# Writing the low part of the dense stages' weight tiles on the vector engine

## The chip, the cores and the metric

The kernel runs on one core of a Trainium2 chip. The metric is the device time of one execution in microseconds (us), the median of several runs. An engine's instructions run in the order in which they stand in its own queue. Between engines they wait on semaphores. PE is the matrix engine (PEld its weight loads), DVE the vector engine, ACT the scalar engine, POOL the GpSimd engine, SP the queue that issues most DMAs.

## The reference

Two layers over 16 learned tokens and 1024 input tokens, width 1024. Layer 0 mixes with multi-head latent attention (16 heads), layer 1 with a causal pooling mixer over windows of 2, 4, 8 and 16 tokens. Each mixer and each gated MLP (inner width 2816) is wrapped in RMS norms. All is float32.

```python
for i in range(DEPTH):
    a = rmsnorm(h, norm_mix_pre[i])
    if i % N_MIXERS == 0:
        m = mla_mixer(a, ...)
    else:
        m = pool_mixer(a, pool_w_group[j], pool_scale[j])
    h = h + rmsnorm(m, norm_mix_post[i])
    f = conv_ffn(rmsnorm(h, norm_ffn_pre[i]), ffn_w_up[i], ffn_conv_w[i], ffn_conv_b[i], ffn_w_down[i])
    h = h + rmsnorm(f, norm_ffn_post[i])
```

In `conv_ffn` an up-projection is followed by a causal depthwise convolution of width 3, `silu(gate) * val`, and a down-projection.

## The kernel before, in words

A matmul reads its operands as `float32r`, which keeps fewer bits than float32. So each float32 operand is split in two: a high part, which is the value rounded to `float32r`, and a low part, which is the value minus the high part. A product is three matmuls: high by high, high by low, low by high. `split` (line 60) makes the two parts. ACT writes the high part (a cast, line 64), and the engine named by `lo_eng` writes the low part with a subtraction (line 70).

The program has two stages. `mla` (the first 550 us or so) computes the latent projections and the attention. `dense` then does the output projection `wo`, the MLP of layer 0, the pooling mixer, and the MLP of layer 1. The 1040 tokens are handled in two halves of 536 and 504 columns (hf 0 and hf 1). Activations stand with the features on the 128 partitions, so the weights are the stationary operand of each matmul.

All weights of `dense` come through `wtile` (line 702). It loads up to 1024 columns of float32 weights into a `wr` tile (three buffers) by a DMA on SP, and splits them into `wh` and `wl` (four buffers each). A tile's `wh` takes the buffer of the tile four before it, so the cast on ACT waits for PE, and the subtraction waits for the cast. `mm_half` (line 744) issues the matmuls (line 756). A half of 536 columns is cut into two matmuls of 268, so a full weight tile is 48 matmuls there and 24 for the half of 504.

In `ffn_up` (line 878) the output of a tile in PSUM is convolved: one ACT pass (line 899), two DVE passes (line 903), then the product of gate and value (line 909) and a split into `gh` and `gl` whose low part is DVE's. In layer 0 with hf 0 the norm's scale comes late, so DVE first copies the PSUM tile times that scale into `u` (line 895). For hf 0 the PSUM pool holds three such tiles, for hf 1 six.

The norms run beside the matmuls as generators in a list `bg`, which `tick` advances between tiles. `post` (line 817) multiplies the eight tiles `F` of a sub-layer's output by gain and scale (line 824), adds them to the residual `H` (line 829), and sums the squares into `acc` (`addsq`, lines 778 and 779). `inv_rms_a` reduces `acc` over the partitions by small matmuls into `ps_st` (line 82), DVE takes the reciprocal root in some dozen tiny instructions (lines 84 to 99), DVE and POOL each write a `diag` tile (line 115), and PE spreads the scale over the partitions into `ps_bc` (line 122), which ACT copies out as `R`. `pre` (line 839) makes the split inputs `ah` and `al` of the next MLP. `poolmix` (line 973) runs four groups of window sums (`pa`, `psm`, `pmx`, lines 988 to 1005), splits the result into `xh` and `xl`, and multiplies by small weights `pwh` and `pwl`, which `wtile` also makes.

The order of the instructions on each engine isn't written by hand: the tile framework's scheduler places each instruction by priority and by its own timeline of when its operands are there. `ahead` lowers a priority number so that norms and mixers go first.

Of the kernel before, what the change touches and what calls it, by code (L numbers as in the profile page):

```python
# [46 lines left out]
class Kern:  # L47
# [654 lines left out]
    def wtile(self, src, nk, pool=False):  # L702
        nc = self.nc
        n = 128 * nk
        r = self.wp.tile([128, 1024], F32, tag="wr", name="wr", bufs=3)
        if pool:
            hi = self.wp.tile([128, 512], F32R, tag="pwh", name="pwh", bufs=1)
            lo = self.wp.tile([128, 512], F32R, tag="pwl", name="pwl", bufs=1)
        else:
            hi = self.wp.tile([128, 1024], F32R, tag="wh", name="wh")  # L710
            lo = self.wp.tile([128, 1024], F32R, tag="wl", name="wl")
        src = src if isinstance(src, list) else [src]
        for i, a in enumerate(src):
            w = n // len(src)
            nc.sync.dma_start(r[:, i * w:i * w + w], a)
        self.split(r[:, :n], hi[:, :n], lo[:, :n])
        return [(hi[:, 128 * k:128 * k + 128], lo[:, 128 * k:128 * k + 128]) for k in range(nk)]

    @staticmethod
# [354 lines left out]
```

## Time and profile before

| | |
|---|---|
| median of 3 runs | 2288.43 us (2287.2 to 2289.56) |
| the profiled execution, its own time | 2289.22 us |
| its span in the trace | 2287.4 us |
| PE busy | 2172.8 us (95%) |
| DVE busy | 1333.4 us (58%) |
| POOL busy | 1124.3 us (49%) |
| ACT busy | 1046.3 us (46%) |
| mean granted PE clock | 0.974 |

Busy time is the union of an engine's instructions, without its register and semaphore work. Durations and waits below come from this one execution; between its span and its own time lie 1.8 us outside the traced instructions.

### The profile page before, as it was taken

The numbers are of one execution on the slowest core, as the hardware profiler recorded it, in microseconds if no ns is written. First come the engines' busy times: TensorE is split into PE (matmuls) and PEld (weight loads), VectorE is DVE, ScalarE is ACT, GpSimd is POOL, SyncE is SP. The second block draws the span as 40 slices with busy tenths as digits, with TensorE's granted clock in tenths as the row PEclk, the third lists the DMA queues.
The fourth block names the chain that finished last, engine by engine and source line by source line (L and its number), as shares of the span: only waits on it lengthen the run. The fifth ranks groups of instructions, "written<-read, shape, count | busy, mean of one in ns | idle before, by whom it ended". The sixth has DMA issues, their size and how long they took to land.

```text
span 2287.4 us, 36601 instructions
## 1 busy us (share of the span) xinstructions
PE 2172.8 (95%) x13968; PEld 1983.4 (87%) x13968; DVE 1333.4 (58%) x2506; ACT 1046.3 (46%) x1934; POOL 1124.3 (49%) x1079
## 2 busy tenths in 40 slices
PE   8889999998989999999998999999899999999996
PEld 8878889887978999999787788899899998888886
DVE  7867777776389614754985534486733347421334
ACT  6456777775454323343443444344334333433431
POOL 5657676765533344444443544444343344444442
PEclk9989999998999999999999999999999999999998
DMA  5011111114343223223222422322242234323231
GB/s 160 16 42 25 32 32 32 26 55 131 120 140 115 85 88 102 89 81 128 80 80 75 149 98 82 130 79 84 60 139 93 79 118 159 113 82 113 96 92 46
DMA packets 82904, 202.77 MB, mean 89 GB/s; under 512 B 10548, under 2 KB 31668, under 8 KB 82728
## 3 DMA queue, kind: packets, MB, share of 16 engines
q1 hardware_dynamic: 82584, 200.18, 27.9%
q8 instruction: 110, 1.80, 0.3%
q14 instruction: 66, 0.54, 0.1%
q10 hardware_dynamic: 144, 0.25, 0.0%
HBM read 179.15 MB, written 16.97 MB: 86 GB/s over the span
## 4 chain that ended last, share of the span: by engine, by line
PE 75%; DVE 13%; ACT 4%; issue 3%; POOL 2%; DMA 2%; SPq 0%; DVEq 0%; ACTq 0%; POOLq 0%
PE ps_m L756 62%; DVE acc L779 2%; PE ps_t L577 2%; DVE cv L903 2%; DVE F L824 1%; PE ps_s L525 1%; PE ps_o L562 1%; PE ps_s L527 1%; PE ps_s L526 1%; DVE H L829 1%; PE ps_o L563 1%; ACT P L540 1%; PE ps_qk L408 1%; DVE psm L998 1%; PE ps_st L82 1%
## 5 line engine op out<-in xcount | busy, mean ns | idle before, releaser
L70 POOL TENSOR_TENSOR wl<-wr,wh 128x1024 fp32r<-128x1024 f32 (+3 forms) x316 | 702.4, 2223 | 891.8 <-ACT wh L64 879.4
L756 PE MATMUL ps_m<-al,wh 128*128 128x506 f32 (+2 forms) x2112 | 569.9, 324 | 0.0
L756 PE MATMUL ps_m<-ah,wh 128*128 128x506 f32 (+2 forms) x2112 | 566.2, 322 | 3.4 <-DVE cv L903 2.5
L756 PE MATMUL ps_m<-ah,wl 128*128 128x506 f32 (+2 forms) x2112 | 566.2, 322 | 0.0
L64 ACT CAST wh<-wr 128x1024 fp32r<-128x1024 f32 (+3 forms) x316 | 300.4, 951 | 502.5 <-PE ps_m L756 351.4
L903 DVE SCALAR_TENSOR_TENSOR cv<-ps_m,params,cv 128x504 f32<-128x504 f32 (+1 forms) x264 | 196.4, 746 | 360.7 <-ACT cv L899 357.1
L756 PEld LDWEIGHTS ps_m<-ah,wh 128*128 128x128 f32 x2112 | 355.5, 191 | 34.2 <-ACT sq L778 2.7
L756 PEld LDWEIGHTS ps_m<-al,wh 128*128 128x128 f32 x2112 | 355.1, 190 | 29.2 <-issue 1.5
L756 PEld LDWEIGHTS ps_m<-ah,wl 128*128 128x128 f32 x2112 | 355.6, 190 | 27.6 <-issue 0.2
L756 PE MATMUL ps_m<-gh,wh 128*128 128x268 f32 (+3 forms) x1088 | 290.4, 319 | 5.0 <-ACT F L765 5.0
L756 PE MATMUL ps_m<-gl,wh 128*128 128x268 f32 (+3 forms) x1088 | 289.7, 319 | 0.0
L756 PE MATMUL ps_m<-gh,wl 128*128 128x268 f32 (+3 forms) x1088 | 289.2, 318 | 0.0
L756 PEld LDWEIGHTS ps_m<-gh,wh 128*128 128x128 f32 x1088 | 184.3, 191 | 19.1 <-ACT F L765 5.2
L756 PEld LDWEIGHTS ps_m<-gh,wl 128*128 128x128 f32 x1088 | 183.6, 190 | 14.3 <-issue 0.5
L756 PEld LDWEIGHTS ps_m<-gl,wh 128*128 128x128 f32 x1088 | 183.6, 190 | 13.4 <-issue 0.2
L64 ACT CAST gh<-cv 128x504 fp32r<-128x504 f32 (+2 forms) x88 | 54.8, 623 | 224.8 <-DVE cv L909 224.8
L779 DVE TENSOR_TENSOR acc<-acc,sq 128x536 f32<-128x536 f32 (+4 forms) x97 | 109.9, 1137 | 50.9 <-ACT sq L778 47.8
L545 POOL TENSOR_SCALAR P<-P,stat 116x116 f32<-116x116 f32 (+2 forms) x144 | 108.7, 756 | 59.2 <-DVE stat L543 47.5
L903 DVE SCALAR_TENSOR_TENSOR cv<-u,params,cv 128x535 f32<-128x535 f32 x88 | 112.4, 1278 | 41.5 <-ACT cv L899 40.2
L907 ACT ACTIVATE cv<-cv 128x504 f32<-128x504 f32 (+2 forms) x88 | 55.9, 635 | 166.8 <-DVE cv L903 166.7
L540 ACT ACTIVATE P<-ps_s,stat 116x116 f32<-116x116 f32 (+9 forms) x160 | 111.3, 698 | 37.5 <-DVE stat L538 26.3
L577 PE MATMUL ps_t<-ident,P 116*116 116x116 f32 x720 | 117.6, 267 | 6.1 <-DVE ptl L591 2.7
(200 smaller groups left out, 3732.9 us busy)
## 6 DMA issues: line engine op xcount, KB each, us to landing
wr<-in_w_up SPq DMA_DIRECT2D x176, 512.0 KB, 3.5
wr<-in_w_down SPq DMA_DIRECT2D x56, 384.0 KB, 3.1
wr<-in_w_down SPq DMA_DIRECT2D x56, 320.0 KB, 2.9
wr<-in_w_o SPq DMA_DIRECT2D x16, 512.0 KB, 3.5
resid<-H SPq DMA_DIRECT2D x16, 268.0 KB, 2.5
H<-resid SPq DMA_DIRECT2D x16, 268.0 KB, 2.8
xt<-in_x SPq DMA_DIRECT2D x32, 130.0 KB, 2.3
resid<-H SPq DMA_DIRECT2D x16, 252.0 KB, 2.4
```

What stands on the lines that cost most here:

```text
L64: nc.scalar.copy(hi, src)
L70: eng.tensor_tensor(lo, src, hi.bitcast(F32), op=ALU.subtract)
L82: nc.tensor.matmul(ps[:w, i:i + 1], acc[:, w * i:w * i + w], self.ones, start=True, stop=True)
L408: nc.tensor.matmul(ps, wh, xh, start=i == 0, stop=False)
L525: nc.tensor.matmul(ps[:n, x, :w], qh[:, qs], kh[:, ks], start=True, stop=False)
L540: nc.scalar.activation(dst, ps, AF.Exp, bias=nm[:n], scale=SCALE, accum_out=es[:n, gi:gi + 1])
L545: nc.gpsimd.tensor_scalar(P[:n, :nk], P[:n, :nk], rs[:n], 1.0, op0=ALU.mult, op1=ALU.mult)
L577: nc.tensor.transpose(pt[:kn, x * QT:x * QT + n], Pi[:n, k0:k0 + kn], self.ident[:n, :n])
L756: nc.tensor.matmul(p, w, x[k][:, skip + c0:skip + c0 + m], start=k == 0 and w is wh and x is xh, stop=k == last and w is wl)
L779: (eng or nc.vector).tensor_tensor(acc, acc, sq[:, :n], op=ALU.add)
L903: nc.vector.scalar_tensor_tensor(c[:, o:], u[:, pad + x - 2 + o:pad + x - 2 + n], self.par(p0 + x), c[:, o:], op0=ALU.mult, op1=ALU.add)
L907: nc.scalar.activation(c, c, AF.Silu)
```

## The change

`wtile` asks `split` for DVE in place of POOL as the engine of the subtraction. This holds for all 324 weight tiles of `dense`: 316 `wl` and 8 `pwl`. The operands, buffers and the arithmetic stay as they are. The other calls of `split`, those of the attention among them, stay as they are too.

```diff
@@ -713,7 +713,7 @@
         for i, a in enumerate(src):
             w = n // len(src)
             nc.sync.dma_start(r[:, i * w:i * w + w], a)
-        self.split(r[:, :n], hi[:, :n], lo[:, :n])
+        self.split(r[:, :n], hi[:, :n], lo[:, :n], lo_eng="dve")
         return [(hi[:, 128 * k:128 * k + 128], lo[:, 128 * k:128 * k + 128]) for k in range(nk)]
```

The scheduler orders the dense stage anew on every engine. Three places follow.

On DVE, the `post` of hf 0 after `wo`, from the tile `diag` to the first rows of `acc`. `F`, `H`, `al` and `acc` are the norm's tiles; the two widths of `acc` belong to the two halves. Before:

```order
L115 TENSOR_TENSOR diag<-ident,yh 67x536
L824 SCALAR_TENSOR_TENSOR F<-F,params,R 128x536 x8
L829 TENSOR_TENSOR H<-H,F 128x536 x8
L866 SCALAR_TENSOR_TENSOR al<-H,params,ah 128x536 x3
L779 TENSOR_TENSOR acc<-acc,sq 128x504
L866 SCALAR_TENSOR_TENSOR al<-H,params,ah 128x536 x5
```

and in the change:

```order
L115 TENSOR_TENSOR diag<-ident,yh 67x536
L70 TENSOR_TENSOR wl<-wr,wh 128x1024
L824 SCALAR_TENSOR_TENSOR F<-F,params,R 128x536 x8
L829 TENSOR_TENSOR H<-H,F 128x536
L70 TENSOR_TENSOR wl<-wr,wh 128x1024
L829 TENSOR_TENSOR H<-H,F 128x536 x7
L70 TENSOR_TENSOR wl<-wr,wh 128x1024
L866 SCALAR_TENSOR_TENSOR al<-H,params,ah 128x536 x3
L779 TENSOR_TENSOR acc<-acc,sq 128x504
L866 SCALAR_TENSOR_TENSOR al<-H,params,ah 128x536
L70 TENSOR_TENSOR wl<-wr,wh 128x1024
L866 SCALAR_TENSOR_TENSOR al<-H,params,ah 128x536 x2
```

From `F` to the last `acc` of this chain six `wl` stand among the norm's instructions now, where none stood, and one more behind it.

On PE, the place where the same chain's `acc` is reduced (`ps_st`, line 82). Before, it stands between the last matmuls of `wo` (`oh`, `ol`) and the first of `ffn_up` (`ah`, `al`):

```order
L756 MATMUL ps_m<-oh,wh 128x504
L756 MATMUL ps_m<-ol,wh 128x504
L756 MATMUL ps_m<-oh,wl 128x504
L82 MATMUL ps_st<-ones,acc 67x1 x8
L756 MATMUL ps_m<-ah,wh 128x268 x2
```

and in the change:

```order
L756 MATMUL ps_m<-ah,wl 128x268 x2
L756 MATMUL ps_m<-ah,wh 128x268 x2
L756 MATMUL ps_m<-al,wh 128x268 x2
L82 MATMUL ps_st<-ones,acc 67x1 x8
L756 MATMUL ps_m<-ah,wl 128x268 x2
```

The reduction moved behind 52 matmuls of `ffn_up`, one weight tile and four matmuls. The next reduction but one (hf 1, `63x1`) moved from the 971st to the 1168th line 756 matmul.

On DVE, the first group of the pooling mixer of hf 0. Before:

```order
L903 SCALAR_TENSOR_TENSOR cv<-ps_m,params,cv 128x504
L998 TENSOR_TENSOR psm<-pa 128x551
L909 TENSOR_TENSOR cv<-cv 128x504
L1001 SCALAR_TENSOR_TENSOR pmx<-psm,pa 128x536
L988 SCALAR_TENSOR_TENSOR pa<-H,params,R 128x536
L1004 TENSOR_TENSOR pmx<-psm,params 128x16
L70 TENSOR_TENSOR gl<-cv,gh 128x504
```

and in the change:

```order
L70 TENSOR_TENSOR gl<-cv,gh 128x504
L998 TENSOR_TENSOR psm<-pa 128x551
L70 TENSOR_TENSOR wl<-wr,wh 128x1024
L1001 SCALAR_TENSOR_TENSOR pmx<-psm,pa 128x536
L988 SCALAR_TENSOR_TENSOR pa<-H,params,R 128x536
L903 SCALAR_TENSOR_TENSOR cv<-ps_m,params,cv 128x504
L1004 TENSOR_TENSOR pmx<-psm,params 128x16
```

A `wl` now stands between the window sum and the `pmx` that the mixer's matmuls wait for.

## Rows read from the trace of the kernel before

**Rows 1.** Page of the profile: span, and busy time of each engine.

```profile
span 2287.4 us, 36601 instructions
PE 2172.8 (95%) x13968; PEld 1983.4 (87%) x13968; DVE 1333.4 (58%) x2506; ACT 1046.3 (46%) x1934; POOL 1124.3 (49%) x1079
```

**Rows 2.** Busy time by stretches: start:end, length, engines (count), PEclk, DMA share, GB/s.

```profile
640.00:740.00 100.00, 86.08 (x620) 81.99 (x618) 85.33 (x131) 45.48 (x67) 42.27 (x17) 0.91 0.34 116
740.00:1090.00 350.00, 350.00 (x2763) 346.19 (x2762) 182.96 (x193) 128.41 (x169) 149.43 (x86) 1.00 0.31 96
1090.00:1290.00 200.00, 185.54 (x865) 153.90 (x864) 150.17 (x218) 87.95 (x140) 97.83 (x58) 0.96 0.30 94
1290.00:1465.00 175.00, 175.00 (x765) 143.98 (x764) 76.06 (x99) 70.90 (x96) 77.23 (x37) 1.00 0.34 108
1465.00:1690.00 225.00, 210.15 (x1585) 200.68 (x1584) 154.69 (x224) 90.74 (x133) 92.96 (x52) 0.96 0.28 86
1690.00:2250.00 560.00, 560.00 (x3302) 499.55 (x3301) 204.32 (x271) 208.98 (x277) 249.32 (x131) 1.00 0.32 104
2250.00:2288.00 38.00, 18.77 (x164) 17.43 (x162) 23.62 (x76) 5.61 (x14) 5.82 (x8) 0.74 0.17 55
```

**Rows 3.** What PE waited for, 590 to 2288 us: total, times, longest, us.

```profile
PE ps_st L82 <- DVE acc L779: 20.6, 5, 8.3
PE ps_m L756 <- ACT xh L64: 10.9, 2, 6.8
```

**Rows 4.** Lines by form, POOL: out<-in, shapes, count | busy us, mean ns | idle before, releaser.

```profile
L70 POOL TENSOR_TENSOR wl<-wr,wh 128x1024 fp32r<-128x1024 f32 x196 | 478.9, 2444 | 590.0 <-ACT wh L64 580.1 <-DMA resid<-H 9.6
L70 POOL TENSOR_TENSOR wl<-wr,wh 128x768 fp32r<-128x768 f32 x56 | 115.8, 2069 | 178.6 <-ACT wh L64 178.6
```

**Rows 5.** Lines by form, DVE (and ACT's cast of the widest weight tile).

```profile
L903 DVE SCALAR_TENSOR_TENSOR cv<-ps_m,params,cv 128x504 f32<-128x504 f32 x176 | 129.9, 740 | 241.4 <-ACT cv L899 239.0
L903 DVE SCALAR_TENSOR_TENSOR cv<-u,params,cv 128x535 f32<-128x535 f32 x44 | 76.3, 1734 | 40.2 <-ACT cv L899 40.2
L903 DVE SCALAR_TENSOR_TENSOR cv<-u,params,cv 128x534 f32<-128x534 f32 x44 | 36.2, 823 | 1.2
L779 DVE TENSOR_TENSOR acc<-acc,sq 128x536 f32<-128x536 f32 x42 | 57.9, 1379 | 32.0 <-ACT sq L778 30.6
L829 DVE TENSOR_TENSOR H<-H,F 128x536 f32<-128x536 f32 x24 | 15.4, 705 | 0.0
L534 DVE CUSTOM_DVE_ANT_0 ps_s<-ps_s,mask 116x928 f32<-116x928 f32 x16 | 18.0, 1128 | 2.7 <-PE ps_s L527 1.3 <-POOL P L545 0.5 <-PE ps_o L563 0.4
L64 ACT CAST wh<-wr 128x1024 fp32r<-128x1024 f32 x196 | 205.5, 1048 | 266.5 <-PE ps_m L756 186.4 <-issue 54.4 <-POOL wl L70 18.0
```

**Rows 6.** Timeline, DVE and then POOL, 622 to 662 us: start us, us, instructions merged.

```profile
622.28 9.88 DVE L824 SCALAR_TENSOR_TENSOR F<-F,params,R 128x536 f32<-128x536 f32 x8 [6.50 <-ACT R L124]
632.08 5.09 DVE L829 TENSOR_TENSOR H<-H,F 128x536 f32<-128x536 f32 x8
...
645.36 14.79 DVE L779 TENSOR_TENSOR acc<-acc,sq 128x504 f32<-128x504 f32 x12
...
623.27 2.72 POOL L70 TENSOR_TENSOR wl<-wr,wh 128x1024 fp32r<-128x1024 f32 x1 [3.80 <-ACT wh L64]
...
654.80 2.60 POOL L70 TENSOR_TENSOR wl<-wr,wh 128x1024 fp32r<-128x1024 f32 x1 [0.17 <-ACT wh L64]
```

**Rows 7.** Timeline, PE, 640 to 672 us: the reduction and the matmuls around it.

```profile
649.33 0.39 PE L756 MATMUL ps_m<-oh,wl 128*128 128x504 f32 x1
658.03 1.97 PE L82 MATMUL ps_st<-ones,acc 128*67 128x1 f32 x16 [8.31 <-DVE acc L779]
```

**Rows 8.** Busy time by stretches, 100 us of layer 0's `ffn_up`, hf 0.

```profile
800.00:900.00 100.00, 100.00 (x812) 100.00 (x812) 24.18 (x23) 31.00 (x41) 42.73 (x22) 1.00 0.31 93
```

**Rows 9.** Busy time by stretches of `wl` alone (PE, PEld, POOL with counts).

```profile
1090.00:1290.00 200.00, 94.50 (x237) 45.92 (x236) 83.58 (x35) 0.96 0.30 94
1465.00:1690.00 225.00, 103.06 (x487) 78.25 (x488) 78.57 (x36) 0.96 0.28 86
```

## The prediction

> **What bounds the kernel now.** I read the page first, then the busy time by stretches, then what PE waited for, then the lines by form, and last the timeline around the longest wait. The page shows PE busy for 95% of the span [rows 1]. In the dense stage the stretches split cleanly: in 740 to 1090, 1290 to 1465 and 1690 to 2250 us PE is busy all the time at clock 1.00 [rows 2]. Nothing that DVE or POOL do there can shorten the kernel. All the dense stage's loss but its tail lies in three stretches where norms and mixers run: 640 to 740, 1090 to 1290 and 1465 to 1690 us. PE sits idle there for 13.9, 14.5 and 14.9 us, and the mean granted clock falls to 0.91, 0.96 and 0.96, so a part of each ran at the lower of the clock's two levels, 1.2 GHz in place of 2.4 [rows 2]. The clock's shares are 9, 8 and 9 us. So these stretches offer at most 22.9 + 22.5 + 23.9 = 69 us.
>
> DVE is busy for 85%, 75% and 69% of them [rows 2], and PE's longest waits name DVE: 20.6 us for `acc` at `ps_st`, 10.9 us for the mixer's `xh`, which ACT casts from DVE's `pmx` [rows 3].
>
> The lines by form then show what slows DVE. The addition `acc` takes 1379 ns on average; the addition `H`, with the same shape and also all in SBUF, takes 705 [rows 5]. The pass of `cv` that reads `u` from SBUF takes 1734 ns, the one behind it 823, and the one that reads PSUM 740. The timeline says why: a DVE instruction with both inputs in SBUF that starts under a POOL `wl` ends when the `wl` ends, and those that read PSUM run on. In 622 to 660 us the eight `F` take 9.9 us, the eight `H`, under no `wl` but one's end, 5.1 us, and twelve `acc` 14.8 us, under `wl` of 2.4 to 3.0 us [rows 6].
>
> **The change, part by part.** *What goes from POOL:* 316 `wl` at 2444 ns for the widest and 2069 for 768 columns [rows 4], and 8 `pwl`. POOL isn't the bound, so its time itself is worth nothing; what counts is the hold on DVE. By groups: `acc` 42 x (1379 - 705) = 28 us, `cv` from `u` 44 x (1734 - 823) = 40 us [rows 5]. The smaller groups look alike, and I estimate 150 us in all.
>
> *What comes to DVE:* no row shows this subtraction on DVE at 1024 columns. From above, 1024/536 times `H`'s 705 ns gives 1347 ns. From below, the 928 columns of the masked maximum take 1128 ns [rows 5], so it isn't under that. Between lies the line through these two points, 705 + (1128 - 705)/392 x 488 = 1232 ns; I take 1.23 us, since 928 is the nearest width. On the same line 768 columns cost 0.96 and 640 cost 0.82 us. The sum is 196 x 1.23 + 56 x 0.96 + 56 x 0.82 = 341 us, and some 14 us for the 16 other tiles: 355 us. DVE's busy time should go from 1333 to about 1333 - 150 + 355 = 1540 us.
>
> *The steady stretches.* A weight tile of 48 matmuls of 268 columns takes PE 48 x 100/812 = 5.9 us [rows 8], and of 24 wide ones about as long (765 matmuls in 175 us, 5.5 us [rows 2]). One more instruction of 1.23 us per tile leaves DVE at some 50 to 75%. `wl` needs the cast, which needs the tile four back to be finished on PE. The DVE work queued right behind it belongs mostly to that finished tile or a later one, so the order adds no wait on PE. Cost nothing, covered by three or more PSUM tiles; if that cover were gone, a late `wl` would cost at most its cast and itself, 1.05 + 1.23 = 2.3 us.
>
> *640 to 740 us.* The chain F, H, al, acc runs from 622.3 to 660.2 us, 37.9 us [rows 6]. Undisturbed, by the pitch of the eight `H` (0.64 us [rows 6]) and 0.74 for the three-operand form as with PSUM [rows 5], it is 16 x 0.74 + 20 x 0.64 = 24.6 us; so POOL's holds cost about 13 us, some 2.2 us for each of six. In the new order six `wl` stand before the last `acc`: 6 x 1.23 = 7.4 us, so 32 us, and the chain ends near 654. The last of those `wl` needs a buffer that PE frees at the end of `wo` (649.3 us [rows 7]) plus the cast, so I say 656. PE now has 52 matmuls of `ffn_up` before the reduction: 52 x 0.123 = 6.4 us past 649.7, or 656. The wait of 8.31 us [rows 7] is gone and with it the slow clock behind it. The reduction of hf 1 is put off by 197 matmuls too, so the second stall should also go. Up to it DVE has 11 `wl`, 12 `u`, 22 `cv`, 9 products and `gl` and 23 wide instructions of the second chain (8 of the dearer form): 11 x 1.23 + 30 x 0.74 + 36 x 0.64 = 59 us, and some tiny ones. PE takes 540 x 0.123 = 66 us for the matmuls before it. It will be close, and some microseconds are lost there. I take 17 of the 22.9 us back; ends 0 and 22.9.
>
> *1090 to 1290 and 1465 to 1690 us.* Here 35 and 36 `wl` start [rows 9]. At 1.2 us (a third of them are narrower: 1.1) they bring some 39 us each to DVE. Their holds are fewer for each, since many of DVE's passes read PSUM there: if every second `wl` holds DVE for 2.2 us, 39 us each, my estimate. So DVE is hardly relieved; the gain is that tiny instructions of the norms no longer stall, that POOL's `diag` no longer queues behind a `wl`, and that PE's reductions stand later. I take 6 us of 22.5 and 6 of 23.9; ends -15 (slower) and +20 each.
>
> *Elsewhere.* At the end of attention three `wl` now stand among DVE's last `ptl`: 3 x 1.23 = 3.7 us more before them, against a POOL hold or two on an `ol`, 2.2 us each, that go. I count +1 us, ends -2 and +4. After 2250 us POOL has 8 instructions [rows 2], none of them a `wl`: 0. DMAs stay on SP; a `wr` buffer is freed when its `wl` is done, 1.2 us faster, or later if DVE is late: 0.
>
> **The sum** against the profiled execution's 2289.2 us: -17 - 6 - 6 + 1 = -28, so 2261 us. The runs shown have their median 0.8 us below that execution, which I leave inside the rounding.
>
> **A rule that speaks against it.** POOL's hold is shown by the rows above. The Trainium skill, "Perfetto Trace Analysis", section "Optimizing Scalar/DVE Operations", says that moving work between GPSIMD and DVE might not help, as they share a read port. Taken strictly, the sum would be no change. The trace agrees on the shared path, but one way costs more: a hold of about 2.2 us against 1.23 us.
>
> **The rivals.** *DVE stalls in its own queue in the mixers (slower).* In 1090 to 1290 and 1465 to 1690 us a `wl` that waits for ACT's cast blocks the window sums behind it. ACT is in order too, and its casts wait for PE 186 us in all [rows 5]. Price: if each of the 71 `wl` costs cast and itself, 2.3 us, that is 163 us, less holds of 78, so 85 us more against 425 - 305 = 120 us of DVE's free time. PE's idle share would then go from 29/425 = 6.9% to the 13.9% of the first stretch [rows 2], 30 us more. With a gain of 14 us in the first stretch: +16, or 2305 us. It decides once DVE, with its waits, is held for over 85% of those stretches. For it: `wl` stands ahead of `pmx` in the new order. Against: the cast waits for the same finished tile as DVE's `cv`, so both come ready together. Chance 0.25.
>
> *The holds are exchanged for work (no change).* The first stretch gains 10, the mixers lose as much: 2289 us. This is the rule above as a mechanism: what DVE is spared it spends. Chance 0.11.
>
> *The scheduler's new order fits everywhere.* With no holds DVE does what the plan assumed, and all three stretches regain most of 69 us: 2289 - 55 = 2234 us. For it: the old order put the reduction where an unheld DVE would have been in time. Against: DVE's load in the mixers doesn't fall. Chance 0.09.
>
> *The change does nothing to POOL's hold.* The order shows no `wl` left on POOL, so I give it none.
>
> **How the numbers follow.** The forecast, 2261 us, has a chance of 0.55, with its own range from 2243 (its gains at 20, 14 and 13) to 2280 us (gains of 12 and little else). A measurement of this kernel can tell about 0.2%, 4.6 us, from no change. Faster by more: 0.55 + 0.09 = 0.64. Within: 0.11. Slower: 0.25. The range for 8 in 10 runs from 2240, with about half of the best case left out, to 2304 us, with about half of the slow case left out.
>
> **What would show it.** Right: `acc` in SBUF near 0.7 us and no `cv` from `u` above 0.8; `wl` on DVE at 1.2 us; DVE near 1540 us busy; no wait of 8 us at `ps_st`; clock near 1.00 in the first stretch; PE idle in the mixers' stretches at 10 to 12 us each. Wrong: PE's waits for `xh` or `acc` grow in the mixers, DVE's idle time before `wl` there is long with ACT's `wh` as releaser, or PE waits for `wl` in a steady stretch.

## The result and the profile after

The changed kernel takes **2250.82 us** (median of 4 runs, 2249.77 to 2252.87). The kernel before, run beside it, takes 2288.99 us (2287.2 to 2289.75). The ratio is 0.9831 with a 95% interval of 0.9819 to 0.9843: 38 us or 1.7% faster. The forecast was 2261 us with a range of 2240 to 2304.

The profiled execution took 2249.77 us, against 2289.22 before: 39.5 us less. The page of the changed kernel:

```profile
span 2247.6 us, 36505 instructions
PE 2154.6 (96%) x13968; PEld 1968.5 (88%) x13968; DVE 1473.8 (66%) x2830; ACT 1048.6 (47%) x1934; POOL 415.5 (18%) x755
```

Against [rows 1] POOL loses 709 us, DVE gains 140 us, and the span falls by 39.8 us. DVE is busier and the kernel faster. By the busy shares alone one would have guessed the opposite.

The busy time by stretches of the changed kernel (columns as in [rows 2]; everything now lies up to 40 us earlier):

```profile
640.00:740.00 100.00, 98.62 (x785) 95.98 (x785) 84.90 (x154) 46.88 (x66) 5.28 (x2) 1.00 0.39 127
740.00:1090.00 350.00, 350.00 (x2677) 341.68 (x2676) 209.09 (x277) 134.75 (x177) 8.02 (x19) 1.00 0.31 96
1090.00:1290.00 200.00, 187.56 (x888) 156.66 (x887) 144.23 (x247) 86.03 (x135) 7.87 (x18) 0.97 0.32 100
1290.00:1465.00 175.00, 175.00 (x846) 146.87 (x845) 104.04 (x144) 69.87 (x94) 1.34 (x1) 1.00 0.33 103
1465.00:1690.00 225.00, 217.30 (x1718) 211.09 (x1717) 156.34 (x248) 95.26 (x140) 8.96 (x11) 0.99 0.31 97
```

Read DVE's column with its counts. In 640 to 740 us DVE is as busy as before (84.9 against 85.3 us), but in that time it finishes 154 instructions where it had finished 131 [rows 2]. In the mixers' stretches it is about as busy (144 against 150 us, 156 against 155), with 247 against 218 and 248 against 224. The busy time that came on top lies in the steady stretches, 209 against 183 and 104 against 76 us, where PE is still busy without a gap. PE's clock in the first stretch is back at 1.00.

The lines by form, DVE, of the changed kernel:

```profile
L70 DVE TENSOR_TENSOR wl<-wr,wh 128x1024 fp32r<-128x1024 f32 x196 | 240.4, 1227 | 267.2 <-ACT wh L64 262.3 <-PE ps_m L756 2.3
L903 DVE SCALAR_TENSOR_TENSOR cv<-ps_m,params,cv 128x504 f32<-128x504 f32 x176 | 129.7, 739 | 2.3
...
L70 DVE TENSOR_TENSOR wl<-wr,wh 128x768 fp32r<-128x768 f32 x56 | 53.6, 957 | 80.7 <-ACT wh L64 74.8 <-PE ps_m L756 5.6
...
L903 DVE SCALAR_TENSOR_TENSOR cv<-u,params,cv 128x534 f32<-128x534 f32 x44 | 34.7, 788 | 1.1
L903 DVE SCALAR_TENSOR_TENSOR cv<-u,params,cv 128x535 f32<-128x535 f32 x44 | 33.9, 772 | 1.0 <-ACT cv L899 0.7
...
L779 DVE TENSOR_TENSOR acc<-acc,sq 128x536 f32<-128x536 f32 x42 | 30.0, 713 | 2.7 <-ACT sq L778 2.2
```

The subtraction takes 1227 ns on DVE, half of POOL's 2444 [rows 4]. `acc` falls from 1379 to 713 ns, the pass of `cv` over `u` from 1734 to 772 [rows 5]. The pass that reads PSUM, which was never held, stays at 739.

What PE waited for in the changed kernel, 550 to 2300 us (total, times, longest):

```profile
PE ps_m L756 <- DVE psm L998: 10.1, 1, 10.1
PE ps_bc L122 <- DVE diag L115: 6.9, 1, 6.9
PE ps_m L756 <- ACT xh L64: 5.0, 2, 2.7
PE ps_m L756 <- ACT F L765: 3.3, 2, 1.9
PE ps_st L82 <- POOL acc L779: 1.9, 1, 1.9
```

The 20.6 us of waits for DVE's `acc` [rows 3] are gone; `diag` and POOL's `acc` belong to the tail. A wait of 10.1 us in the pooling mixer is now the longest.

The start of the same matmul in both traces shows where the 39.8 us come from. I number the 10,320 line 756 matmuls and compare the starts of the 576th, 1400th, 3938th, 5000th and 7500th, which in the trace of before stand at 649.3, 777.5, 1112.9, 1372.0 and 1761.1 us. Every column of this table is such a difference, a profiled execution minus the kernel before's, in us per stretch; the runs below the first are those of the experiments.

| run | to 576th | to 1400th (first) | to 3938th (steady) | to 5000th (mixer, hf 0) | to 7500th (mixer, hf 1) |
|---|---|---|---|---|---|
| the change | -3.0 | -18.1 | 0.0 | -5.1 | -13.6 |
| e1, POOL reads two | +1.4 | +7.4 | +15.7 | +24.2 | +10.8 |
| e2, POOL reads one | +0.7 | -18.1 | 0.0 | -2.9 | -10.8 |
| e12, POOL reads none | -1.4 | -18.1 | 0.0 | -5.0 | -13.5 |
| e3, DVE by flag | -0.5 | -16.2 | 0.0 | -0.6 | -7.0 |
| e4, the reverse | -1.1 | -0.2 | 0.0 | -3.4 | -2.8 |
| e5, DVE by place | -1.6 | -18.1 | 0.0 | -5.2 | -9.9 |
| e6, DVE twice | +1.9 | -8.3 | +1.3 | +26.1 | -4.4 |
| e7, pooling on POOL | -0.7 | -18.1 | 0.0 | -5.3 | -14.0 |
| e8, mixers on POOL | -0.5 | -18.1 | 0.0 | -5.2 | -10.0 |

The -3.0 of the first column isn't the change's. The 2400th matmul of the program, in the attention stage, already starts at 391.6 us against 394.7, 3.1 us earlier, although PE, DVE, ACT and POOL have the same instructions in the same order up to 543 us; over the profiled executions of all the kernels it lies between 391.6 and 395.5 us. So it is scatter between two executions. From there to the 576th matmul the changed kernel gains 0.0. Only e1, e2 and e6 stand apart in this stretch, with 3.1, 1.9 and 3.1 us more than the kernel before. What the change brings in these two executions is then 36.8 us, in the first stretch and the two mixers.

The first stretch ends as the forecast's chain had it. The changed kernel's DVE in 646 to 656 us, and PE's reduction:

```profile
647.56 1.22 DVE L70 TENSOR_TENSOR wl<-wr,wh 128x1024 fp32r<-128x1024 f32 x1 [2.12 <-ACT wh L64]
648.70 4.53 DVE L779 TENSOR_TENSOR acc<-acc,sq 128x536 f32<-128x536 f32 x7
```

```profile
654.60 1.08 PE L82 MATMUL ps_st<-ones,acc 128*67 128x1 f32 x16
```

Twelve `acc` had taken 14.8 us [rows 6]; here seven take 4.5 us. The last of hf 0 ends at 651.9, and PE reaches the reduction at 654.6 and doesn't wait, where it had waited 8.31 us [rows 7]. Two things cover that wait. Counted from the start of the 576th matmul, hf 0's last `acc` ends after 5.6 us, where it had ended after 8.7: the chain itself brings 3.1 us. The other 5.2 us are covered because the new order has 52 matmuls ahead of the reduction.

### The profile page after: what moved, and what is told of

The parts are those of the page before. It is cut to its first block, busy times and chain, and to the rows that moved or that the text cites. A ratio compares the mean times of both kernels' runs of the same rounds, so it can differ in the third digit from the quotient of the medians.

```text
span 2247.6 us, 36505 instructions
## 1 busy us (share of the span) xinstructions
PE 2154.6 (96%) x13968; PEld 1968.5 (88%) x13968; DVE 1473.8 (66%) x2830; ACT 1048.6 (47%) x1934; POOL 415.5 (18%) x755
## 4 chain that ended last, share of the span: by engine, by line
PE 85%; DVE 6%; ACT 3%; POOL 2%; issue 2%; DMA 2%; DVEq 0%; SPq 0%; ACTq 0%; POOLq 0%
PE ps_m L756 72%; PE ps_t L577 2%; PE ps_s L525 1%; PE ps_o L562 1%; PE ps_o L563 1%; PE ps_s L527 1%; PE ps_s L526 1%; ACT P L540 1%; PE ps_qk L408 1%; POOL P L545 1%; PE ps_qk L410 1%; DMA xt<-in_x 1%; PE ps_qk L409 1%; PE ps_st L82 1%; DVE ps_s L534 1%
## 5 line engine op out<-in xcount | busy, mean ns | idle before, releaser
L70 DVE TENSOR_TENSOR wl<-wr,wh 128x1024 fp32r<-128x1024 f32 (+3 forms) x316 | 349.3, 1105 | 419.6 <-ACT wh L64 408.6
L115 POOL TENSOR_TENSOR diag<-ident,yl 65x260 fp32r<-65x260 f32 (+5 forms) x27 | 33.5, 1241 | 714.5 <-DVE yl L70 675.3
L534 DVE CUSTOM_DVE_ANT_0 ps_s<-ps_s,mask 116x116 f32<-116x116 f32 (+7 forms) x128 | 89.9, 704 | 22.6 <-PE ps_s L527 12.1
```

The source lines that it names most:

```text
L70: eng.tensor_tensor(lo, src, hi.bitcast(F32), op=ALU.subtract)
L115: eng.tensor_tensor(t, self.ident[:w, :w].unsqueeze(1).broadcast_to([w, n, w]), part.bitcast(F32).unsqueeze(2).broadcast_to([w, n, w]), op ...
L534: nc.vector.tensor_tensor_reduce(out=ps, in0=ps, in1=self.mask[:n, o:o + nb * cn].rearrange("p (b c) -> p b c", b=nb), op0=ALU.add, op1=AL ...
```

## The experiments

The theory: POOL's `wl` holds DVE's instructions on SBUF, and lifting this hold shortens DVE's chain where that chain sets PE. Rival A: the scheduler's new order alone did it, with PE's reductions later. Rival B: the low part is ready 1.2 us sooner. Every kernel below starts from the changed kernel and is scheduled anew. PE's order stays near the changed kernel's in e1, e2, e3, e5, e7 and e12; in e4 it is nearly that of the kernel before, and e6 and e8 to e11 have orders of their own. Ratios are to the kernel before, with 95% intervals.

### POOL reads two, one or no inputs behind DVE's subtraction

```diff
-        self.split(r[:, :n], hi[:, :n], lo[:, :n], lo_eng="dve")
+        self.split(r[:, :n], hi[:, :n], lo[:, :n], lo_eng="dve"); nc.gpsimd.tensor_tensor(r[:, :n], hi[:, :n].bitcast(F32), lo[:, :n].bitcast(F32), op=ALU.add)
```

> Behind the changed kernel's subtraction on DVE, POOL adds hi and lo of every weight tile back into the landing tile, an addition with two inputs in SBUF that no one on PE, ACT or DVE waits for. The order on the other engines stays nearly that of the changed kernel and the low part is still ready after 1.2 us. Theory (the gain came from lifting POOL's hold): the holds come back, acc near 1.3 us and the pass of cv over u near 1.7 us in place of 0.71 and 0.77, DVE busy over 1650 us in place of 1474, and since DVE now carries both the holds and the subtraction, the time is at or over the kernel before's: 2285 to 2320 us. Rival A (the gain came from the new order, in which PE's reductions stand later) and rival B (it came from the shorter subtraction, 1.2 us in place of 2.4): DVE's instructions may be slow, but the time stays within 10 us of 2251.

In place of the addition, `nc.gpsimd.tensor_scalar(r[:, :n], lo[:, :n].bitcast(F32), 1.0, 0.0, op0=ALU.mult, op1=ALU.add)`:

> As the run before, but POOL's extra instruction reads one input only (the low part times 1 plus 0, written into the landing tile). It takes POOL's time and the landing tile's release as in that run. Theory: what holds DVE is two inputs read from SBUF on both sides at once; if one input on POOL is enough to hold, acc is again near 1.3 us and the time over 2280; if not, acc stays at 0.71 us and the time within 5 us of 2251. I expect the second with 0.6. Rivals A and B: 2251 either way. If this run is fast and the two-input one slow, the late release of the landing tiles is ruled out as the cause of the difference.

And, run last, `nc.gpsimd.memset(r[:, :n], 0.0)`:

> The third of the series behind DVE's subtraction: POOL only writes zeros into the landing tile and reads nothing from SBUF. The two-input addition stretched the pass of cv over u under it from 0.76 us to 2.5 on average, the one-input copy to 1.3. Theory: what holds DVE is POOL's reading of SBUF, so here cv over u stays under 0.8 us, acc at 0.71, DVE busy at 1474 us or near it, and the time within 4 us of 2251. Rival: any POOL instruction on SBUF holds DVE while it lasts; then cv over u is over 1.0 us and the time over 2255.

Two inputs (e1): 2349.24 us, ratio 1.0258 (1.0243 to 1.0274). One input (e2): 2259.21 us, 0.9870 (0.9854 to 0.9887). None (e12): 2252.28 us, 0.9843 (0.9829 to 0.9856). PE's order is nearly the changed kernel's in all three. The forms, first POOL's widest, then DVE's pass of `cv` over `u` that stands behind a `wl`; of the two-input run:

```profile
L716 POOL TENSOR_TENSOR wr<-wh,wl 128x1024 f32<-128x1024 f32 x196 | 509.4, 2600 | 601.8 <-DVE wl L70 526.3 <-issue 72.7 <-DVE ahalo L70 2.8
...
L903 DVE SCALAR_TENSOR_TENSOR cv<-u,params,cv 128x534 f32<-128x534 f32 x44 | 91.5, 2080 | 1.1
```

of the one-input run:

```profile
L716 POOL TENSOR_SCALAR wr<-wl 128x1024 f32<-128x1024 f32 x196 | 242.3, 1237 | 789.6 <-DVE wl L70 697.2 <-issue 77.0 <-DVE nv L84 5.0
...
L903 DVE SCALAR_TENSOR_TENSOR cv<-u,params,cv 128x534 f32<-128x534 f32 x44 | 51.8, 1177 | 1.1
```

and of the run without input:

```profile
L716 POOL MEMSET wr<- 128x1024 f32 x196 | 187.0, 954 | 845.3 <-DVE wl L70 733.7 <-issue 70.1 <-DVE nv L84 15.5
...
L903 DVE SCALAR_TENSOR_TENSOR cv<-u,params,cv 128x534 f32<-128x534 f32 x44 | 34.7, 788 | 1.1
```

The same DVE instruction takes 2080, 1177 and 788 ns. DVE's busy time is 1733.6, 1528.1 and 1474.2 us; the changed kernel has 1473.8. So POOL costs DVE nothing when it only writes, 54 us of busy time when it reads one input, and 260 us when it reads two. This decides against A and B as the whole cause: with the changed order and the low part just as early, a POOL instruction that reads two inputs turns a gain of 38 us into a loss of 59. It doesn't tell how the 38 us divide between the lifted hold and the new order; that the order has a share, the first stretch above shows.

Two expectations missed in size. I gave the two-input run at most 2320 us. In it ACT's casts also waited for POOL to be done with `wh`, 60 us in all, 29.5 of them for the widest tiles (the kernel before has 18.0 there [rows 5], the run without input none). So its 97 us over that run are hold and that wait together. The trace separates a part: all of these waits lie behind 1290 us, and at the 3938th matmul, at 1137 us, the two-input run is already 44 us behind the run without input. At least these 44 us are without ACT's wait. Of the one-input run I expected all or nothing. It holds too, but only while its 1.24 us last, and in the first stretch, which has room for that, it costs nothing.

### Where the subtraction's engine matters

```diff
+        self.split(r[:, :n], hi[:, :n], lo[:, :n], lo_eng="dve" if self.bg else "pool")
```

> The subtraction is on DVE only for weight tiles that are issued while norms or mixers are interleaved with the dense stage (112 tiles), on POOL for the other 212. Theory: all the gain lies in the stretches where DVE's chain sets PE, so nearly all of it stays: 2249 to 2260 us, with DVE's busy time about 230 us lower than the changed kernel's less the holds that return in steady stretches. If the relief in the steady stretches matters as well, it comes out above 2265.

```diff
+        self.split(r[:, :n], hi[:, :n], lo[:, :n], lo_eng="pool" if self.bg else "dve")
```

> The reverse: POOL has the subtraction for the 112 tiles that are issued while norms or mixers run, DVE has it for the other 212, which is most of the work that the change moves. Theory: back to the kernel before, 2280 to 2295 us. Rival B (a shorter subtraction everywhere) expects some two thirds of the gain, 2263 us.

By flag (e3): 2263.35 us, 0.9883 (0.9868 to 0.9898), between the two expectations, so it settled nothing by itself. The trace says why: the flag goes by where a tile is asked for, and in 1090 to 1290 and 1465 to 1690 us still 23 and 21 low parts ran on POOL. There the table shows -0.6 and -7.0 in place of -5.1 and -13.6.

The reverse (e4): 2282.9 us, 0.9970 (0.9958 to 0.9981), as the theory had it. 212 of 324 subtractions are on DVE, two thirds, and the gain is a fifth. That speaks against B, which asked for 2263. The first stretch has its 8.3 us wait for `acc` back.

So I placed them by number (e5):

```diff
+        i = self.nw; self.nw += not pool; self.split(r[:, :n], hi[:, :n], lo[:, :n], lo_eng="dve" if pool or 11 <= i < 34 or 98 <= i < 138 or 170 <= i < 213 else "pool")
```

> The run with DVE only under norms missed its aim: its flag goes by where a tile is asked for, and in the mixers' stretches 23 of 35 and 21 of 38 low parts still ran on POOL. Here the tile's number decides: DVE for the 106 tiles whose subtraction fell in the changed kernel's 610 to 740, 1087 to 1290 and 1465 to 1690 us and for the 8 pooling tiles, POOL for the other 210. Theory (the hold costs only where DVE's chain sets PE): the changed kernel's time, 2246 to 2256 us, although two thirds of the low parts are still on POOL. Rival (something in the steady stretches or the tail matters too): 2263 us or more.

2256.39 us, 0.9863 (0.9846 to 0.9879): just above the range for the theory, well under the rival's 2263. With 114 of 324 subtractions on DVE it keeps 33.2 of the change's 36.8 us (by the medians 32.5 of 38.2). The first stretch and the first mixer gain just as much; 3.7 us are missing in the second mixer. DVE's busy time is 1338.8 us, 5 us over the kernel before's. So most of the gain is bought in three stretches, and the steady ones add nothing to it either way.

### What the added work costs DVE

```diff
+        self.split(r[:, :n], hi[:, :n], lo[:, :n], lo_eng="dve")
+        nc.vector.tensor_tensor(lo[:, :n], r[:, :n], hi[:, :n].bitcast(F32), op=ALU.subtract)
```

> DVE does the subtraction of every weight tile twice, which adds some 350 us of busy time to it and no work to POOL. It prices what the change adds. The second instruction makes the low part ready 1.2 us later, as late as on POOL. If DVE's added work has room, as the forecast had it for steady stretches, the time grows only where DVE's chain sets PE: 17 tiles of 1.2 us in the first stretch, 35 and 39 in the mixers', at most 91 x 1.15 = 105 us, and I expect a third of that, 2285 us (2260 to 2310). Per tile a hold in the two-inputs run cost (2349 - 2259)/324 = 0.28 us; if this run is under 2340, a subtraction on DVE costs less than a hold.

The doubled subtraction (e6): 2305.62 us, ratio 1.0076 (1.0061 to 1.0091): 55 us over the changed kernel, half of the ceiling, not the third I expected. The table shows where: 9.8 us in the first stretch, 31.2 in the first mixer, 9.2 in the second, 1.3 in the steady stretch; 3.1 more fall at the end of attention. What PE waited for in its 1090 to 1290 us:

```profile
PE ps_m L756 <- ACT xh L64: 28.0, 4, 11.8
PE ps_bc L122 <- DVE diag L115: 8.9, 1, 8.9
```

This is where the slow rival had it: DVE's work in the mixer comes late, and PE waits for `xh`. Most of the added work is paid for in the first mixer: 35 more subtractions are some 39 us by the forecast's count. Per tile a second subtraction costs 55/324 = 0.17 us of the kernel's time, and a two-input POOL instruction 97/324 = 0.30 us, with the later readiness in the one and ACT's wait in the other. By stretches, and as far as two different orders can be compared, the hold is dearer in the first stretch (25.5 against 9.8 us) and in the steady one (15.7 against 1.3), where ACT doesn't wait for POOL; in the first mixer the two cost about the same (29.2 against 31.2).

### The wait of 10 us that is new

In the changed kernel PE stops at 1183.3 us, before the fourth pooling group of hf 0, and resumes at 1193.4. Its DVE, 1177 to 1186 us:

```profile
1177.80 0.72 DVE L70 TENSOR_TENSOR xl<-pmx,xh 128x536 fp32r<-128x536 f32 x1 [0.71 <-ACT xh L64]
1181.38 0.83 DVE L70 TENSOR_TENSOR wl<-wr,wh 128x640 fp32r<-128x640 f32 x1 [2.86 <-ACT wh L64]
1182.12 1.52 DVE L903 SCALAR_TENSOR_TENSOR cv<-ps_m,params,cv 128x504 f32<-128x504 f32 x2
1183.67 0.68 DVE L909 TENSOR_TENSOR cv<-cv 128x504 f32<-128x504 f32 x1
1184.27 0.68 DVE L70 TENSOR_TENSOR pwl<-wr,pwh 128x512 fp32r<-128x512 f32 x1
1184.87 0.77 DVE L988 SCALAR_TENSOR_TENSOR pa<-H,params,R 128x536 f32<-128x536 f32 x1
```

DVE stands idle for 2.86 us at a `wl` whose cast on ACT isn't there yet, and the fourth group's first `pa` is queued behind it. Before, `pa` started 6.0 us ahead of PE's stop (1201.8 against 1207.8 us); now it starts 1.6 us behind it. Five runs bear on this wait. The first two put low parts back on POOL:

```diff
+        self.split(r[:, :n], hi[:, :n], lo[:, :n], lo_eng="pool" if pool else "dve")
```

> Only the 8 pooling tiles' low part goes back to POOL. In the changed kernel the longest wait of PE, 10.1 us, ends with the fourth pooling group, and its first step pa stood on DVE behind the pooling tile's subtraction, which waits for ACT's cast and so for the group before on PE. There the changed kernel lost 5.4 us against the kernel before. Theory (a DVE queue stuck behind a subtraction that waits, my slow rival in small): PE's wait falls to 6 or 8 us and the time to some 2246 us. Otherwise pa is held by something else, and the time stays within 2 us of 2251.

The pooling tiles back on POOL (e7): 2251.63 us, 0.9841 (0.9826 to 0.9855). No gain, so the second alternative. PE still waits 10.5 us, since `pa` remains behind the `wl` and the `cv` of the matmul tile, and POOL's `pwl` now holds `pa` for 1.78 us.

```diff
+        self.mixing = True; F, acc = yield from self.poolmix(hf, R); self.mixing = False
...
+        self.split(r[:, :n], hi[:, :n], lo[:, :n], lo_eng="pool" if self.mixing else "dve")
```

> All low parts that are asked for while the mixers run (26, the 8 pooling tiles among them) go back to POOL. If DVE's queue stuck behind subtractions costs more there than POOL's holds, the time falls below the run with pooling tiles alone, to 2244 us; if the holds cost more, it rises to 2254 us or more. I lean to the second, 0.6.

All 26 low parts asked for in the mixers on POOL (e8): 2255.94 us, 0.9858 (0.9843 to 0.9873), the side I leaned to. In the first mixer it is a draw (-5.2 against -5.1), in the second it costs 3.6 us. So there a hold and a subtraction come to about the same, as far as this run with its own order tells: the forecast's no-change rival, in one place.

Then I let the mixer itself end sooner. One step less between two groups, one less between a group's channels, and both (e9, e10 and e11):

```diff
-            yield
+            if g == 3: yield
```

> On the changed kernel, the mixer's step between two pooling groups goes: a group's first pa is asked for with the group before's matmuls and not one step later, so the mixer ends three steps sooner and the fourth group's pa stands on DVE ahead of the subtractions and cv that wait for PE. In the changed kernel DVE sat idle for 2.9 us at such a subtraction with this pa behind it, and PE then waited 10.1 us, with 10.2 us at the slow clock behind it, some 15 us in all. If that queue is the reason, PE's wait there falls under 4 us and the time to 2238 to 2245 us. If the mixer's own chain on DVE is simply too long, the wait moves to another group and the time stays within 4 us of 2251.

```diff
-                    W = self.wtile(io["w_pool"][g], 4, True)
-                yield
+                    W = self.wtile(io["w_pool"][g], 4, True); yield
```

> The same aim in another place: the step between the two channels of a pooling group goes, so the mixer ends four steps sooner. Same expectation, 2238 to 2246 us; if DVE's work bunched by this delays the cv that free PE's PSUM tiles, PE waits for cv and the time rises over 2251.

> Both steps go, seven in all. If one of them is enough, no better than the better of the two; if DVE's bunched work now delays cv, worse than both by 3 us or more.

All three are slower than the changed kernel, where I had expected 2238 to 2246 us of the first two: 2267.5 us (0.9905, 0.9891 to 0.9918), 2274.0 us (0.9929, 0.9917 to 0.9942) and 2292.54 us (1.0014, 1.0005 to 1.0023). In the first of them one wait of 10.1 us became three, of 4.3, 7.8 and 7.1 us, before three of the groups. Its DVE in 1155 to 1189 us shows why:

```profile
1155.23 0.72 DVE L70 TENSOR_TENSOR xl<-pmx,xh 128x536 fp32r<-128x536 f32 x1 [0.70 <-ACT xh L64]
1163.42 1.23 DVE L70 TENSOR_TENSOR wl<-wr,wh 128x1024 fp32r<-128x1024 f32 x1 [7.47 <-ACT sq L778]
1164.57 0.71 DVE L779 TENSOR_TENSOR acc<-acc,sq 128x536 f32<-128x536 f32 x1
1165.20 0.69 DVE L70 TENSOR_TENSOR pwl<-wr,pwh 128x512 fp32r<-128x512 f32 x1
1165.80 0.77 DVE L988 SCALAR_TENSOR_TENSOR pa<-H,params,R 128x536 f32<-128x536 f32 x1
...
1179.83 0.72 DVE L70 TENSOR_TENSOR xl<-pmx,xh 128x536 fp32r<-128x536 f32 x1 [0.70 <-ACT xh L64]
1186.53 0.69 DVE L70 TENSOR_TENSOR pwl<-wr,pwh 128x512 fp32r<-128x512 f32 x1 [5.99 <-ACT pwh L64]
1187.46 0.72 DVE L779 TENSOR_TENSOR acc<-acc,sq 128x536 f32<-128x536 f32 x1 [0.23 <-ACT sq L778]
1188.09 0.77 DVE L988 SCALAR_TENSOR_TENSOR pa<-H,params,R 128x536 f32<-128x536 f32 x1
```

DVE is idle for 7.47 and 5.99 us with the next group's `pa` in its queue. `pa` now stands ahead of some of the `wl` and `cv`, but behind `acc` and `pwl` of the group before. Both wait for ACT, and ACT for PE's matmuls of that group: `acc` needs their output, and `pwh` has one buffer. So the mechanism is the one I supposed, DVE stuck in its own queue, but this edit put other waiting instructions ahead of `pa` and made it worse; whether the same happens in the other two runs isn't shown. To take them all away at once, `pwl`, `acc` and `wl`, wasn't tried, and no version here beat the changed kernel.

## Why the forecast was right, and where it was off

*The bound and the mechanism* were right. Without lifting the hold there is no gain: the series of POOL instructions with two, one and no inputs shows it with PE's order nearly fixed. The forecast also counted on the reduction's later place, and needed it; the two shares weren't measured apart over the whole kernel.

*What comes to DVE* was right: 1.23 us for 1024 columns and 0.96 for 768, as forecast. *What goes* was too small. DVE's busy time rose to 1473.8 us and not to 1540. With 349 us of `wl` and some 6 us of `pwl` added, the holds removed are 1333.4 + 355 - 1473.8 = 215 us, where I estimated 150 from the groups that I had looked at.

*640 to 740 us*, -17: measured -18.1. The chain, the reduction at 656 (654.6 measured, 657.7 without the 3.1 us of scatter) and the clock (1.00) came as worked out. I left 5.9 us of the 22.9 to the second stall, but that sum was too large: it adds the clock's share to the idle time, and while PE stood idle, 8.3 us at a mean clock of 0.75 and 5.3 us at 0.93, some 2.4 us of the clock's share fell into the idle time itself. Of the 20.5 us that were there, nearly all came back.

*The first mixer*, -6 of 22.5: measured -5.1, but as a sum of parts that I hadn't seen, so the good agreement is partly luck. At its start, where a wait of 3.8 us for `acc` is gone, the changed kernel gains 6.6 us. By the first matmul of the fourth pooling group, the 4345th, all but 0.1 us of this is lost again. The other 5 come behind it, most of them where the second wait for `acc`, 2.2 us, had been.

*The second mixer*, -6 of 23.9: measured -13.6. This is the term that was mis-sized, and 7.6 of the 11 us by which the sum missed; another 3 are the scatter of the first column. I reckoned in totals there, so much hold against so much work, and called DVE "hardly relieved". Busy time is indeed the same, 156 against 155 us. But the holds sat on the chains that PE waited for. Some 5.5 us of the 13.6 come behind the mixer, in the norm of hf 1. DVE's eight `F` and PE's wait, before:

```profile
1652.33 8.19 DVE L824 SCALAR_TENSOR_TENSOR F<-F,params,R 128x504 f32<-128x504 f32 x8 [3.86 <-ACT R L124]
1662.30 0.80 PE L756 MATMUL ps_m<-gh,wh 128*128 128x260 f32 x2 [5.00 <-ACT F L765]
```

and in the changed kernel:

```profile
1617.75 5.32 DVE L824 SCALAR_TENSOR_TENSOR F<-F,params,R 128x504 f32<-128x504 f32 x8 [2.61 <-ACT R L124]
1624.85 0.51 PE L756 MATMUL ps_m<-gh,wh 128*128 128x260 f32 x2 [1.90 <-ACT F L765]
```

Behind these eight stands DVE's first `H`, behind that a square of `H` on ACT, and behind this, in ACT's queue, the copy `F` (line 765) that PE waits for. The wait falls from 5.00 to 1.90 us, and the mean clock behind it, from 1662.3 to 1670 us, had been 0.65; now it is 1.00. Another 4.6 us come at the reduction at 1516.8 us, where PE had waited for an `acc` that took 2.8 us. The fourth pooling group of hf 1 is worth some 2 us, but there one sees the holds singly. In the kernel before, DVE:

```profile
1615.42 1.79 DVE L988 SCALAR_TENSOR_TENSOR pa<-H,params,R 128x504 f32<-128x504 f32 x1
1617.31 2.05 DVE L998 TENSOR_TENSOR psm<-pa 128x519 f32<-128x519 f32 x1
...
1623.86 2.02 DVE L988 SCALAR_TENSOR_TENSOR pa<-H,params,R 128x504 f32<-128x504 f32 x1
```

and its POOL:

```profile
1615.38 1.29 POOL L70 TENSOR_TENSOR pwl<-wr,pwh 128x512 fp32r<-128x512 f32 x1 [4.44 <-ACT pwh L64]
...
1617.24 1.56 POOL L70 TENSOR_TENSOR wl<-wr,wh 128x640 fp32r<-128x640 f32 x1
1623.26 2.08 POOL L70 TENSOR_TENSOR wl<-wr,wh 128x640 fp32r<-128x640 f32 x1 [4.46 <-ACT wh L64]
```

The changed kernel's DVE in the same place:

```profile
1583.40 0.74 DVE L988 SCALAR_TENSOR_TENSOR pa<-H,params,R 128x504 f32<-128x504 f32 x1
...
1584.65 0.70 DVE L998 TENSOR_TENSOR psm<-pa 128x519 f32<-128x519 f32 x1
...
1588.63 0.82 DVE L70 TENSOR_TENSOR wl<-wr,wh 128x640 fp32r<-128x640 f32 x1 [0.63 <-ACT wh L64]
...
1589.96 0.74 DVE L988 SCALAR_TENSOR_TENSOR pa<-H,params,R 128x504 f32<-128x504 f32 x1
```

Three steps that took 5.86 us take 2.18, and one `wl` of 0.82 us comes between. PE's idle time in this stretch fell to 7.7 us, where I had said 10 to 12; in the first mixer it is 12.4.

*The end of attention*, +1: measured 0.0, once the scatter ahead of it is taken off. I counted three `wl` against a hold or two; in the trace they come out even.

*The steady stretches*, 0: measured 0.0 in all runs but the two-input and the doubled one.

*The rule.* The Trainium skill, "Perfetto Trace Analysis", section "Optimizing Scalar/DVE Operations", would have it that moving work between the two engines might not help, since they share a read port. The runs agree that the two get in each other's way, and show where the two directions aren't equal. The chain of the first stretch, from the first `F` to the last `acc`, took 37.9 us and now takes 34.0, of which 7.3 are six `wl` and 2.1 a wait for ACT. That leaves 24.6 us, so six POOL `wl` had cost it 13.3 us, 2.2 each, against 1.2 us of work. Over the whole kernel it is the other way round: 355 us of work came for 215 us of hold. The move pays by where the holds fell, not in total.

*The rivals.* The slow one is real but small at this load: it takes some 6 us ahead of one pooling group. With the subtraction doubled, or with both steps of the mixer gone, it comes to 28 us of waits for `xh` and makes the kernel as slow as before or slower. The no-change one, a hold exchanged for as much work, is seen in the first mixer alone (e8). The third, that all three stretches regain most of 69 us, came out for the first stretch only: together they regained 36.8.

## What to carry to other kernels

Before weighing two engines by busy share, look whether one's instructions grow longer under the other's: two forms of the same shape with different means, or one line that takes 0.7 us with PSUM and 1.7 with SBUF, are the sign. Then price the hold where it falls on the chain that PE waits for, not in total: here 35% of the moves brought some nine tenths of the gain. Work added to the relieved engine is free only while other engines' work covers it, and before a step is moved forward one should look which waiting instructions of its queue will then stand ahead of it.

## What the runs showed of the hardware

A held DVE instruction ends later than I had read it: in the rows of 1615 to 1626 us above it ends 0.54, 0.56 and 0.54 us behind the end of the POOL instruction, not far from its whole own time of 0.7 us, as if most of its work began only when POOL's ended. The hold goes both ways: in the two-input run a POOL addition that started at 631.17 us, among DVE's additions `H`, took 7.66 us, where such additions take 2.60 on average. DVE ran seven `H` and a `wl` one behind the other at their usual 0.71 and 1.22 us meanwhile, and only the next, an `al`, was held, for 2.92 us. So not every DVE instruction under a POOL one is held. POOL's copy with one input holds DVE too, but it lasts 1.24 us where two inputs take 2.60. A POOL instruction that only writes, 0.95 us each, holds nothing: the pass of `cv` over `u` took 0.78 us under it on average and 0.77 clear of it. The Trainium skill, "SBUF — State Buffer", section "SBUF: two separate sides", has the two engines share a pair of ports that one of them holds as an exclusive lock for its whole instruction, with DVE's two-input forms locked out only by a GpSimd operation that reads SBUF. The runs agree, as far as times can: 2080 ns on average behind two inputs, 1177 behind one, 788 behind none.
